# Two fused network blocks in float32 on one core: small tiles moved to pools behind the others

## The chip, the cores and the metric

The kernel runs on one NeuronCore of a Trainium2 chip. The metric is the time of one execution on the device, in microseconds (us); the time of a kernel is the median of several executions. Before the change three executions took 3017.45, 3017.50 and 3017.97 us.

## The reference, cut to what matters

Two blocks follow each other on 512 tokens of 1024 features (and 256 tokens of context in the first). All of it is float32.

```python
# block 1 (one layer): modulation, one wide projection, delta-rule heads and window pooling, output product
proj = (rms_norm(x) * (1 + scale) + shift) @ w_in
o    = delta_rule(q, k, v, g, beta)            # 8 heads, chunks of 128 tokens, forward and backward
y    = concat([o * silu(z_dn), pool(u) * silu(z_pool)])
x    = x + gate * (y @ w_out)
# block 2 (two layers l)
h = h + 0.5 * swiglu(rmsnorm(h), w_ff1_in[l], w_ff1_out[l])
h = h + hybrid_mixer(rmsnorm(h), ...)          # attention and a convolution of 31 taps, gated, then w_out
h = h + 0.5 * swiglu(rmsnorm(h), w_ff2_in[l], w_ff2_out[l])
h = h + sigmoid(rmsnorm(h) @ w_ple_gate[l]) * (p[l] @ w_ple_proj[l])
```

Most of the work is dense products of activations with weights.

## The kernel before

**The dense product.** Activations lie with features on the 128 partitions and 512 tokens along the free axis, so one tile is 512 float32 values, 2048 bytes, in each partition. TensorE multiplies them in the type fp32r. To keep float32's accuracy each factor is split into a high and a low part, and one 128 x 128 block of weights costs three matmuls of 512 columns (`mm3`, L153 to L158):

```python
    nc.tensor.matmul(ps, lhsT=wh, rhs=xh, start=start, stop=False)   # L156
    nc.tensor.matmul(ps, lhsT=wh, rhs=xl, start=False, stop=False)   # L157
    nc.tensor.matmul(ps, lhsT=wl, rhs=xh, start=False, stop=stop)    # L158
```

The weights (`lhsT`) are loaded into the array, one weight load per matmul; the activations (`rhs`, here called the moving operand) stream through it.

**The weights.** The class Stream brings them in the order of their use, 8 blocks (512 KB) to a DMA into a tile `wraw` (three buffers, L98 and L99), and splits 4 blocks at a time: ACT casts the high part `whi` (L108), DVE subtracts for the low part `wlo` (L109), three buffers each. So 12 matmuls of `mm3` go with one cast and one subtraction, and 24 with one DMA.

**The order.** [...] Block 1 projects and runs the heads one after another; the head before is worked on while the next one is projected (the letters of `STEPS`), then comes the pooling half (`TAIL`), then the output product (`wo`, L1501). Block 2 is, for each of two layers: a first feed-forward (products into `pj`, then per half eight products into `fo`, L352), the mixer, a second feed-forward, and the `ple` product with its gates. Short matmuls in plain float32 (128 columns, for the delta rule and the attention) run between the dense ones in block 1's heads and in block 2's attention.

**Moving operands of the dense products, by name.** `xh`, `xl` (pool `xp` of the whole kernel) are what most of block 2's products into `pj` and all projections `px` of block 1 read. `gh`, `gl` (pool `gp` of block 2, L341 and L342) feed `fo`. `nh`, `nl` (pool `mp` of block 2) take the place of `xh`, `xl` in one feed-forward only, the first one of layer 1 (`prep` with `alt=True`, L640): there the same lines of code multiply with operands that lie elsewhere. `mh`, `ml`, `oh`, `ol`, `ph`, `pl` lie in `gp`, `yh`, `yl` in `mp`. In block 1 `os` (L1489, split at L1494), `ysp`, `yl` and `dsp` feed `wo` and `py`; they lie in its pool `b1c`.

**Where tiles lie.** A pool hands out a fixed stretch of each partition's memory; pools follow each other in the order in which they are opened, and each tile's size is rounded up to 32 bytes. The pools of the whole kernel (`cp`, `wp`, `hp`, `xp`, L1516 to L1519) end at byte 97,792 of the partition, which is 191 x 512. There the pools of block 1 begin, and after block 1 has ended those of block 2, over the same bytes. The built program lists these places (start byte, and its remainder by 512):

| tiles | pool | start bytes | remainder by 512 |
|---|---|---|---|
| `wraw`, `whi`, `wlo` | wp | 24,064 to 46,592 | 0 |
| `xh`, `xl` | xp | 65,024 to 95,744 | 0 |
| `nh`, `nl`, `yh`, `yl` (block 2) | mp | 131,488 to 162,208 | 416 |
| `gh`, `gl`, `mh`, `ml`, `oh`, `ol`, `ph`, `pl` | gp | 164,256 to 207,264 | 416 |
| temporaries `fa`, `fb` and others, tag `t` | tp | 213,408 to 223,648 | 416 |
| `R` (block 2) | b2c | 114,880 and 116,928 | 192 |
| `os`, `ysp`, `dsp`, `yl` (tags P, Q, QK) | b1c | 120,672 to 151,392 | 352 |
| `os` (tags E and B, two operands) | b1c | 178,656 to 188,384 | 480 |

The remainders come from small tiles in front. In block 2 the pool `cp` (L182) mixes tiles of 512 bytes and more with tiles of 16 and 32 bytes (`fv`, `fr`, `ts`, `Rt`, `sm`, `lv`, `lr`, 13 buffers of 32 bytes each, together 416), and the pools `mp`, `gp` and `tp` follow it. In block 1 `cp` (L803) mixes likewise (`par1`, `modv`, the gate columns, the padded inputs `u0` to `u3` of 3096 bytes and others), and `tp` (L804) follows it. A weight block inside `whi` or `wlo` starts at a multiple of 512.

Of the kernel before, what the change touches and what calls it, by code (L numbers as in the profile page):

```python
# [7 lines left out]
F32 = mybir.dt.float32  # L8
F32R = mybir.dt.float32r
# [4 lines left out]
P = 128  # L14
S = 512
D = 1024
KD = D // P
# [3 lines left out]
GRP = 8  # L21
UNIT = 4
# [60 lines left out]
class Stream:  # L83
    """Weight tiles in the order of their use: loads of GRP tiles, split in units of UNIT tiles."""
# [40 lines left out]
    def group(self, dst):  # L125
        """the next GRP tiles as they are"""
        assert self.i % GRP == 0
        self.nc.sync.dma_start(dst, self.dram[self.i // GRP])
        self.i += GRP
# [31 lines left out]
def split_scaled(nc, hi, lo, src, scale):  # L161
    """hi + lo == src * scale (scale: a value per partition)."""
    nc.scalar.activation(hi, src, AF.Copy, scale=scale)
    nc.vector.scalar_tensor_tensor(lo, src, scale, hi.bitcast(F32), op0=ALU.mult, op1=ALU.subtract)
# [12 lines left out]
def block2(tc, kk, W, h, xp, x0, sq0, p_t, par, out_t):  # L177
    """h: 8 tiles [128, 512] (features on partitions), short of the factor 1 / rms of the block before.
    x0: the first operand, split. sq0: the sums of squares for that factor and for the first norm."""
    nc = tc.nc  # L180
    with ExitStack() as ctx:
# [3 lines left out]
        tp = ctx.enter_context(tc.tile_pool(name="b2t", bufs=1))  # L185
        acc = ctx.enter_context(tc.tile_pool(name="b2a", bufs=BANKS2[0], space=PSUM))
# [18 lines left out]
        # second operands of the scores, double buffered, for the two heads of a pair:  # L205
        # upper q and ones; lower k and both parts of the decay sums
# [9 lines left out]
        # mt[q, k] = NEG where k > q  # L216
# [60 lines left out]
        def token_sums(sq):  # L277
            """means of squares with a token per partition, [128, chunk]"""
            ps = paux("ts", (P, 8))
            for t in range(4):  # L280
                nc.tensor.matmul(ps[:, 2 * t:2 * t + 2], lhsT=sq[:, t * P:t * P + P], rhs=kk.ones[1024][:, 0:2],
                                 start=True, stop=True)
            return ps[:, ::2]

        def token_rstd(r, v):
            s = cp.tile([P, 4], F32, tag="ts", name="ts", bufs=2)
            nc.scalar.activation(s, v, AF.Sqrt)
            nc.vector.reciprocal(r, s)
            nc.vector.scalar_tensor_tensor(s, r, -0.5, r, op0=ALU.mult, op1=ALU.mult)
            nc.vector.tensor_tensor(s, v, s, op=ALU.mult)  # L290
            nc.vector.scalar_tensor_tensor(r, s, 1.5, r, op0=ALU.add, op1=ALU.mult)

        def spread(r):
            """from a token per partition to tokens along the free axis of every partition"""
# [6 lines left out]
        def first_norm():  # L301
            """1 / rms of the block before times the first norm's factor; and the former for h"""
            v = [cp.tile([P, 4], F32, name=f"fv{i}") for i in range(2)]
            r = [cp.tile([P, 4], F32, name=f"fr{i}") for i in range(2)]
# [55 lines left out]
        def mixer(l, after):  # L360
# [8 lines left out]
            def qk_steps(hp, qk1):  # L369
                """for either head: (upper | lower) q and (upper | upper) k"""  # L370
# [56 lines left out]
            def taps(n):  # L427
                """the next n of the products that are possible by now"""
# [7 lines left out]
            def heads(hp, qk1, filler):  # L436
                """heads 2 hp and 2 hp + 1, each in its half of the partitions"""
# [7 lines left out]
                for qb in range(4):  # L445
# [9 lines left out]
                    for i, ps in enumerate(pss):  # L455
                        o = ps[:, :n]
                        nc.tensor.matmul(ps[:, qs], lhsT=kk.identr, rhs=maskr, start=False, stop=True)
                        sm = cp.tile([P, 4], F32, tag="sm", name="sm", bufs=4)
# [32 lines left out]
            # token sums of squares per partition, for the token-major values  # L491
# [4 lines left out]
            Rt = cp.tile([P, 8], F32, tag="Rt", name="Rt")  # L496
            rstd(Rt, pst)
            # v, token-major
# [12 lines left out]
            # forget gates: rows 0..7 and again 64..71  # L511
# [9 lines left out]
            # -log_sigmoid = ln(1 + exp(-|z|)) - min(z, 0)  # L521
# [35 lines left out]
            # the merge: gates run ahead of the two parts  # L557
# [84 lines left out]
        v = cp.tile([P, 4], F32, name="lv")  # L642
        r = cp.tile([P, 4], F32, name="lr")
# [10 lines left out]
def blocks(v, n):  # L654
    """[..., n * 128] -> [128, ... * n]"""
# [35 lines left out]
NX = 512  # L691
# [7 lines left out]
# (shift, scale) blocks that are computed together  # L699
# [98 lines left out]
def block1(tc, kk, W, h, xp, hp, xt, ctxt, par1, po, rcnt, prep2):  # L798
    """Fills h (8 tiles [128, 512]) with the block's output before its final norm is applied, times the
    final gain; prep2(m) is called for each one. Returns the sums of squares for both norms."""  # L800
    nc = tc.nc
    with ExitStack() as ctx:
        cp = ctx.enter_context(tc.tile_pool(name="b1c", bufs=1))  # L803
        tp = ctx.enter_context(tc.tile_pool(name="b1t", bufs=1))  # L804
        dp = ctx.enter_context(tc.tile_pool(name="b1d", bufs=2, space=bass.MemoryType.DRAM))
# [4 lines left out]
        par = cp.tile([P, par1.shape[1]], F32, name="par1")  # L810
# [28 lines left out]
        # ---- constants  # L839
# [6 lines left out]
        for d in range(2):  # L846
            t = tmp("tri", (P, P))
            # d = 0: 1 where row <= col; d = 1: 1 where row >= col
# [7 lines left out]
        for b in (16, 32, 64):  # L856
            # -1 on the two off-diagonal blocks of every pair of b x b blocks
# [13 lines left out]
        # row selector: column r picks rows r and 64 + r  # L871
        zs = cp.tile([80, 16], F32R, name="zsel")
# [16 lines left out]
        # ---- modulation vectors, [128, block, (x, ctx)]  # L889
        # (x, ctx) of every input tile, the last ones filled up to a column tile  # L890
        cm = cp.tile([P, 2 * KD + 30], F32, name="cm")
# [3 lines left out]
        # sums over the four column tiles, whose first two rows count  # L895
        sum4 = cp.tile([P, 2], F32, name="sum4")
# [4 lines left out]
        modv = cp.tile([P, 24, 2], F32, name="modv")  # L901

        def modulation(bs, tiled, tiles):
            """four blocks; tiled: with the inputs spread over four column tiles"""
# [19 lines left out]
        # ---- load x, ctx; sums of squares; scale by the reciprocal rms  # L924
# [21 lines left out]
        def newton(r, v, s):  # L946
            """r = 1 / sqrt(v) to float32's accuracy from an estimate r; s: scratch"""
# [4 lines left out]
        def squares(i):  # L952
            R, n = raw[i], (NX, NCX)[i]
            sq = cp.tile([P, NT + 6], F32, tag=f"u{n // NX}", name="sq")[:, :n]
# [24 lines left out]
        A = cp.tile([P, KD, 2], F32, name="A")  # L979
# [48 lines left out]
        # ---- gates: per token on partitions, [128, chunk, 2 directions x 8 heads]  # L1028
# [9 lines left out]
        def gcol(name):  # L1038
            return cp.tile([P, 6, 16], F32, name=name)
# [3 lines left out]
        ea = cp.tile([P, 16], F32, name="ea")  # L1043
# [24 lines left out]
        Gr = cp.tile([P, 6, 16], F32R, name="Gr")  # L1068
# [10 lines left out]
        # ---- per head  # L1079
        # tokens with two columns of zeros around each sequence: ctx from 2 on, x from 260 on  # L1080
        us = {}
        for i in range(4):
            u = cp.tile([P, NT + 6], F32, tag=f"u{i}", name=f"u{i}")
# [5 lines left out]
        def conv5(px, pc, blk, dst):  # L1089
            """centred convolution over tokens, then silu; dst: [128, NT + 2] (a gap after ctx) or [128, NX],  # L1090
            None: left in the input's place"""
# [10 lines left out]
            t = tp.tile([P, NT + 2], F32, tag="cv", name="cv", bufs=1)[:, :n]  # L1102
# [14 lines left out]
        def k_in(hd):  # L1117
# [10 lines left out]
            ss = cp.tile([P, 4, 6], F32, tag="ssk", name="ssk", bufs=2)  # L1128
# [14 lines left out]
            # gamma and its product with the decay to the chunk's end, [128, chunk, direction]  # L1143
            st.ga = cp.tile([P, 2, 6, 2], F32, tag="ga", name="ga", bufs=2)
# [18 lines left out]
        def q_in(st):  # L1163
# [9 lines left out]
            st.sq = cp.tile([P, 4], F32, tag="ssq", name="ssq", bufs=2)  # L1173
            # 128 eps (|q|^2 + eps)
            nc.vector.tensor_scalar(st.sq, pq[:, 0:8:2], EPS, P * EPS, op0=ALU.add, op1=ALU.mult)

        def pre(st):
            """The triangular systems' matrices, forward above the diagonal and backward below it, and the
            inverses of their 16 x 16 diagonal blocks."""
# [30 lines left out]
            # one block per partition: forward ones transposed from 0 on, backward ones from 64 on  # L1210
# [9 lines left out]
            # X: the forward inverse's transpose, the backward inverse  # L1220
            XT = tmp("XT")[0:112, :256].rearrange("p (r c) -> p r c", c=16)
            nc.vector.tensor_copy(XT, X.rearrange("p r c -> p c r"))
            # inverses (backward | forward) and their transposes (forward | backward)
# [20 lines left out]
        def merge(st):  # L1244
            """Doubles the inverted blocks three times. With the blocks 1 and 2 of a pair, for B upper triangular
            (forward) and lower triangular (backward) in one matrix:
            P12 = -P11 B12 P22 (forward), P21 = -P22 B21 P11 (backward), Q: the transposes."""
            for b in (16, 32, 64):
                g = 64 // b

                def alt(t, c):
                    """columns of blocks 1 of each pair from the first matrix, of blocks 2 from the second"""
# [78 lines left out]
        def finish(st, z):  # L1331
            f = cp.tile([P, 4, 4], F32, tag="f", name="f", bufs=2)
# [44 lines left out]
        # ---- pooling half  # L1377
# [5 lines left out]
        ups = [cp.tile([P, NT + 6], F32, tag=f"u{2 + e}", name="up")[:, :640].rearrange("p (r c) -> p r c", c=80) for e in range(2)]  # L1383
# [4 lines left out]
        rns = [tp.tile([P, 14, 64], F32, tag="cv", name="rn0", bufs=1),  # L1388
# [12 lines left out]
        def pool_in(g):  # L1401
            """differences to the window means of group g"""
# [3 lines left out]
            for e in range(2):  # L1406
# [3 lines left out]
                # along the columns: into the middle rows  # L1410
# [11 lines left out]
                if w == 16:  # L1422
                    # all eight rows
# [5 lines left out]
                else:  # L1429
                    # row r of the grid: row r + 4 of rows, row r + 3 of the partial sums  # L1430
# [55 lines left out]
        # ---- delta-rule half  # L1486
# [90 lines left out]
```

## Time and profile before

| what | value |
|---|---|
| median of three executions | 3017.5 us |
| lowest and highest | 3017.45 and 3017.97 us |
| span of the profiled execution (first to last instruction) | 3016.3 us |
| PE (matmuls) busy | 2970.0 us, 98% of the span, 13,980 instructions |
| PEld (weight loads) busy | 2395.5 us, 79% |
| DVE busy | 1916.6 us, 64% |
| ACT busy | 1302.3 us, 43% |
| TensorE clock granted, mean over the span | 0.995 of full speed |
| DMA | 268.77 MB, mean 89 GB/s |

The profile is of one execution; what lies between its span and the median is 1.2 us. Matmuls overlap in the profile: each has a duration of some 0.39 us, but in a dense run a new one starts every 0.23 us. What a matmul costs is therefore read from the distance between starts, not from its duration. A plain float32 matmul appears as two instructions (two passes), an fp32r one as one.

### The profile page before, as it was taken

What the parts mean: (1) busy time and instruction counts of PE and PEld (TensorE: products, weight loads), DVE (VectorE), ACT (ScalarE), POOL (GpSimd) and SP (SyncE); (2) the same over time, 40 slices, a digit from 0 to 9 for tenths busy, and PEclk for the clock granted to TensorE, in tenths of its full rate; (3) what the DMA queues carried; (4) which work ended last, traced back from release to release, by engine and by line L of the source; (5) the groups of instructions that cost most, each with busy time, mean ns of one, the idle gap of its engine ahead of it and who ended that gap; (6) DMA issues with size and microseconds to landing.
All of it is one profiled execution on the core that took longest, in us unless ns stands there. A gap on an engine that the chain in (4) does not pass through costs nothing.

```text
span 3016.3 us, 37957 instructions
## 1 busy us (share of the span) xinstructions
PE 2970.0 (98%) x13980; PEld 2395.5 (79%) x13980; DVE 1916.6 (64%) x3778; ACT 1302.3 (43%) x2395; POOL 48.4 (2%) x105
## 2 busy tenths in 40 slices
PE   7999999999999999999999999999999999999998
PEld 4888887777888887688888878888887688888886
DVE  5788888777534469886543447434469886543446
ACT  5667666435323335544332335323335544432333
POOL 1000000000000000000000000000000000000000
PEclk9999999999999999999999999999999999999999
DMA  5211113232232232133333333323222123233322
GB/s 199 66 46 45 52 51 110 91 91 89 93 98 97 92 98 78 50 92 97 94 95 98 98 98 93 96 91 98 91 93 89 50 85 98 93 96 98 98 91 84
DMA packets 112971, 268.77 MB, mean 89 GB/s; under 512 B 43537, under 2 KB 47121, under 8 KB 112785
## 3 DMA queue, kind: packets, MB, share of 16 engines
q1 hardware_dynamic: 111760, 266.28, 28.3%
q8 instruction: 110, 1.80, 0.2%
q14 instruction: 77, 0.62, 0.1%
q0 software_dynamic: 1024, 0.07, 0.0%
HBM read 262.17 MB, written 4.06 MB: 88 GB/s over the span
## 4 chain that ended last, share of the span: by engine, by line
PE 95%; DVE 2%; ACT 2%; issue 1%; DMA 0%; DVEq 0%; SPq 0%; ACTq 0%
PE pj L158 17%; PE pj L157 17%; PE pj L156 17%; PE fo L158 5%; PE fo L157 5%; PE fo L156 5%; PE px L156 3%; PE px L157 3%; PE px L158 3%; PE o L484 1%; PE wo L157 1%; PE wo L158 1%; PE mP L1266 1%; PE mX L1261 1%; PE wo L156 1%; PE chn L1313 1%
## 5 line engine op out<-in xcount | busy, mean ns | idle before, releaser
L108 ACT CAST whi<-wraw 128x512 fp32r<-128x512 f32 x914 | 566.6, 620 | 1191.9 <-PE pj L157 712.2
L109 DVE TENSOR_TENSOR wlo<-wraw,whi 128x512 fp32r<-128x512 f32 x914 | 627.1, 687 | 465.9 <-ACT whi L108 441.8
L157 PE MATMUL pj<-xl,whi 128*128 128x512 f32 x1712 | 673.0, 393 | 0.0
L156 PE MATMUL pj<-xh,whi 128*128 128x512 f32 x1712 | 670.7, 392 | 0.9 <-DVE h L1502 0.9
L158 PE MATMUL pj<-xh,wlo 128*128 128x512 f32 x1712 | 670.0, 391 | 0.0
L158 PEld LDWEIGHTS pj<-xh,wlo 128*128 128x128 f32 x1712 | 322.1, 188 | 68.1 <-issue 2.3
L157 PEld LDWEIGHTS pj<-xl,whi 128*128 128x128 f32 x1712 | 322.2, 188 | 67.9 <-issue 2.7
L156 PEld LDWEIGHTS pj<-xh,whi 128*128 128x128 f32 x1712 | 322.4, 188 | 66.8 <-ACT whi L108 1.3
L158 PE MATMUL fo<-gh,wlo 128*128 128x512 f32 x704 | 279.1, 396 | 0.0
L157 PE MATMUL fo<-gl,whi 128*128 128x512 f32 x704 | 279.1, 396 | 0.0
L156 PE MATMUL fo<-gh,whi 128*128 128x512 f32 x704 | 279.0, 396 | 0.0
L418 DVE SCALAR_TENSOR_TENSOR cy<-ca,par,cy 128x489 f32<-128x489 f32 (+17 forms) x240 | 169.6, 729 | 1.5
L157 PE MATMUL px<-xl,whi 128*128 128x512 f32 x392 | 160.4, 409 | 0.0
L158 PE MATMUL px<-xh,wlo 128*128 128x512 f32 x392 | 160.0, 408 | 0.0
L156 PE MATMUL px<-xh,whi 128*128 128x512 f32 x392 | 159.3, 406 | 0.0
L157 PEld LDWEIGHTS fo<-gl,whi 128*128 128x128 f32 x704 | 132.6, 188 | 32.3
L156 PEld LDWEIGHTS fo<-gh,whi 128*128 128x128 f32 x704 | 132.6, 188 | 32.3
L158 PEld LDWEIGHTS fo<-gh,wlo 128*128 128x128 f32 x704 | 132.6, 188 | 32.3
L339 DVE TENSOR_TENSOR fb<-pj,R 128x512 f32<-128x512 f32 x88 | 60.8, 691 | 131.5 <-PE pj L158 131.5
L336 DVE TENSOR_TENSOR fa<-pj,R 128x512 f32<-128x512 f32 x88 | 60.8, 691 | 127.4 <-PE pj L158 125.5
L156 PE MATMUL pj<-nh,whi 128*128 128x512 f32 x352 | 140.0, 398 | 0.0
L157 PE MATMUL pj<-nl,whi 128*128 128x512 f32 x352 | 139.5, 396 | 0.0
(431 smaller groups left out, 4499.0 us busy)
## 6 DMA issues: line engine op xcount, KB each, us to landing
wraw<-in_w_dram SPq DMA_DIRECT2D x465, 512.0 KB
mw<-in_w_dram SPq DMA_DIRECT2D x16, 512.0 KB
raw<-in_xt_dram SPq DMA_DIRECT2D x8, 256.0 KB
h<-in_xt_dram SPq DMA_DIRECT2D x8, 256.0 KB
out_dram<-fin SPq DMA_DIRECT2D x8, 256.0 KB
rawc<-in_ctxt_dram SPq DMA_DIRECT2D x2, 512.0 KB
db<-B SPq DMA_DIRECT2D x64, 6.0 KB
Pm<-dq SPq DMA_DIRECT2D x64, 12.0 KB
```

The source lines that it names most:

```text
L108: nc.scalar.copy(hi, src)
L109: nc.vector.tensor_tensor(lo, src, hi.bitcast(F32), op=ALU.subtract)
L156: nc.tensor.matmul(ps, lhsT=wh, rhs=xh, start=start, stop=False)
L157: nc.tensor.matmul(ps, lhsT=wh, rhs=xl, start=False, stop=False)
L158: nc.tensor.matmul(ps, lhsT=wl, rhs=xh, start=False, stop=stop)
L336: nc.vector.tensor_tensor(a, pa, R, op=ALU.mult)
L339: nc.vector.tensor_tensor(b, pb, R, op=ALU.mult)
L418: nc.vector.scalar_tensor_tensor(yy[:, s:], ca[cb][:, :S - s], pcol("conv_w", l, cb, j), yy[:, s:], op0=ALU.mult, op1=ALU.add)
L484: nc.tensor.matmul(po_[r, kb * P:], lhsT=vt[kb][:, hp * P + 64 * i:hp * P + 64 * i + 64], rhs=pts[i], start=kb == 0, stop=kb == 3)
L1261: nc.tensor.matmul(pX[:, o], lhsT=st.B[:, m0 + m], rhs=alt(st.Q, m0 + m), start=True, stop=True)
L1266: nc.tensor.matmul(pP[:, o], lhsT=Xt[:, m], rhs=alt(st.P, m0 + m), start=True, stop=True)
L1313: nc.tensor.matmul(pa, lhsT=st.kN[:, c], rhs=y2, start=True, stop=True)
```

## The change

Two new pools `sp` are opened behind the other SBUF pools of block 1 and of block 2, and every tile whose size in a partition is no multiple of 512 bytes takes its memory from there. The instructions, their order and the sizes of all tiles stay as they were. (Comments and docstrings are also dropped from the file; they are left out here.)

```diff
 def block2(tc, kk, W, h, xp, x0, sq0, p_t, par, out_t):
         tp = ctx.enter_context(tc.tile_pool(name="b2t", bufs=1))
+        sp = ctx.enter_context(tc.tile_pool(name="b2s", bufs=1))
...
-            s = cp.tile([P, 4], F32, tag="ts", name="ts", bufs=2)
+            s = sp.tile([P, 4], F32, tag="ts", name="ts", bufs=2)
...
-            v = [cp.tile([P, 4], F32, name=f"fv{i}") for i in range(2)]
-            r = [cp.tile([P, 4], F32, name=f"fr{i}") for i in range(2)]
+            v = [sp.tile([P, 4], F32, name=f"fv{i}") for i in range(2)]
+            r = [sp.tile([P, 4], F32, name=f"fr{i}") for i in range(2)]
...
-                        sm = cp.tile([P, 4], F32, tag="sm", name="sm", bufs=4)
+                        sm = sp.tile([P, 4], F32, tag="sm", name="sm", bufs=4)
...
-            Rt = cp.tile([P, 8], F32, tag="Rt", name="Rt")
+            Rt = sp.tile([P, 8], F32, tag="Rt", name="Rt")
...
-        v = cp.tile([P, 4], F32, name="lv")
-        r = cp.tile([P, 4], F32, name="lr")
+        v = sp.tile([P, 4], F32, name="lv")
+        r = sp.tile([P, 4], F32, name="lr")
...
 def block1(tc, kk, W, h, xp, hp, xt, ctxt, par1, po, rcnt, prep2):
         tp = ctx.enter_context(tc.tile_pool(name="b1t", bufs=1))
+        sp = ctx.enter_context(tc.tile_pool(name="b1o", bufs=1))
...
-        par = cp.tile([P, par1.shape[1]], F32, name="par1")
+        par = sp.tile([P, par1.shape[1]], F32, name="par1")
...
-            u = cp.tile([P, NT + 6], F32, tag=f"u{i}", name=f"u{i}")
+            u = sp.tile([P, NT + 6], F32, tag=f"u{i}", name=f"u{i}")
...
-            t = tp.tile([P, NT + 2], F32, tag="cv", name="cv", bufs=1)[:, :n]
+            t = sp.tile([P, NT + 2], F32, tag="cv", name="cv", bufs=1)[:, :n]
...
```

In block 1 the same is done to `zsel`, `cm`, `sum4`, `modv`, `sq`, `A`, the gate columns, `ea`, `Gr`, `ssk`, `ga`, `ssq`, `f`, `up` and `rn0`. The pools of the whole kernel are not touched.

## Rows read from the trace of the kernel before

**Rows 1.** The page: span, busy time of the engines, chain that ended last by engine.
```profile
span 3016.3 us, 37957 instructions
...
PE 2970.0 (98%) x13980; PEld 2395.5 (79%) x13980; DVE 1916.6 (64%) x3778; ACT 1302.3 (43%) x2395; POOL 48.4 (2%) x105
...
PE 95%; DVE 2%; ACT 2%; issue 1%; DMA 0%; DVEq 0%; SPq 0%; ACTq 0%
```
**Rows 2.** The page's costliest groups: xcount | busy us, mean ns | idle before, releaser.
```profile
L108 ACT CAST whi<-wraw 128x512 fp32r<-128x512 f32 x914 | 566.6, 620 | 1191.9 <-PE pj L157 712.2
L109 DVE TENSOR_TENSOR wlo<-wraw,whi 128x512 fp32r<-128x512 f32 x914 | 627.1, 687 | 465.9 <-ACT whi L108 441.8
L157 PE MATMUL pj<-xl,whi 128*128 128x512 f32 x1712 | 673.0, 393 | 0.0
...
L157 PE MATMUL fo<-gl,whi 128*128 128x512 f32 x704 | 279.1, 396 | 0.0
...
L157 PE MATMUL pj<-nl,whi 128*128 128x512 f32 x352 | 139.5, 396 | 0.0
```
**Rows 3.** Timeline of PE, layer 0's first feed-forward: start us, duration, instruction.
```profile
780.05 0.39 PE L157 MATMUL pj<-xl,whi 128*128 128x512 f32 x1
...
839.89 0.39 PE L157 MATMUL pj<-xl,whi 128*128 128x512 f32 x1
```
**Rows 4.** Timeline of PE, layer 1's first feed-forward.
```profile
1899.72 0.39 PE L157 MATMUL pj<-nl,whi 128*128 128x512 f32 x1
...
1979.85 0.40 PE L157 MATMUL pj<-nl,whi 128*128 128x512 f32 x1
```
**Rows 5.** Windows holding rows 3 and 4: us, busy (xcount) by engine, PEclk, DMA share, GB/s.
```profile
760.00:840.00 80.00, 80.00 (x359) 66.37 (x358) 41.64 (x65) 27.41 (x45) 0.00 (x0) 1.00 0.29 93
...
1880.00:1990.00 110.00, 110.00 (x471) 88.41 (x470) 53.05 (x81) 37.35 (x60) 0.00 (x0) 1.00 0.29 92
```
**Rows 6.** Timeline of PE, the products into fo of layer 0's first feed-forward.
```profile
859.87 0.39 PE L157 MATMUL fo<-gl,whi 128*128 128x512 f32 x1
...
899.93 0.39 PE L157 MATMUL fo<-gl,whi 128*128 128x512 f32 x1
```
**Rows 7.** Timeline of PE, block 1's output product.
```profile
700.05 0.40 PE L158 MATMUL wo<-os,wlo 128*128 128x512 f32 x1
...
723.87 0.39 PE L158 MATMUL wo<-os,wlo 128*128 128x512 f32 x1
```
**Rows 8.** Timeline of PE, the switch from wo to px in block 1's pooling half.
```profile
606.36 0.39 PE L156 MATMUL px<-xh,whi 128*128 128x512 f32 x1
...
608.67 0.39 PE L157 MATMUL px<-xl,whi 128*128 128x512 f32 x1
```
**Rows 9.** Groups of PE by line and form: xcount | busy us, mean ns | idle before.
```profile
L157 PE MATMUL px<-xl,whi 128*128 128x512 f32 x392 | 160.4, 409 | 0.0
...
L157 PE MATMUL pj<-ml,whi 128*128 128x512 f32 x128 | 50.7, 396 | 0.0
...
L156 PE MATMUL wo<-ysp,whi 128*128 128x512 f32 x64 | 25.6, 410 | 1.2 <-ACT ysp L168 1.1
...
L157 PE MATMUL pj<-yl,whi 128*128 128x512 f32 x64 | 25.4, 396 | 0.0
...
L157 PE MATMUL pj<-ol,whi 128*128 128x512 f32 x64 | 25.4, 396 | 0.0
...
L158 PE MATMUL wo<-os,wlo 128*128 128x512 f32 x64 | 25.3, 395 | 0.0
```
**Rows 10.** Timeline of PE: runs of plain float32 passes, weights off and on a multiple of 512.
```profile
301.32 0.83 PE L1266 MATMUL mP<-Pm,Xt 128*128 128x128 f32 x6
...
729.46 0.95 PE L281 MATMUL ts<-ones,sq 128*128 128x2 f32 x8
```
**Rows 11.** Timeline of PE where block 2 begins.
```profile
726.67 0.39 PE L158 MATMUL wo<-os,wlo 128*128 128x512 f32 x1
727.99 0.47 PE L156 MATMUL pj<-xh,whi 128*128 128x512 f32 x1 [0.94 <-DVE h L1502]
```

More of the change, by code (lines that the diff above doesn't have):

```diff
@@ L870, in block1 @@
         nc.vector.memset(onesm, 1.0)
-        zs = cp.tile([80, 16], F32R, name="zsel")
+        zs = sp.tile([80, 16], F32R, name="zsel")
         zt = tmp("zt", (80, 16))
@@ L887, in block1 @@
             DD.append((lt, xx))
-        cm = cp.tile([P, 2 * KD + 30], F32, name="cm")
+        cm = sp.tile([P, 2 * KD + 30], F32, name="cm")
         nc.vector.memset(cm, 0.0)
@@ L894, in block1 @@
             nc.scalar.activation(cm[:, i:2 * KD:2], pcol(nme, 0, 8), AF.Silu)
-        sum4 = cp.tile([P, 2], F32, name="sum4")
+        sum4 = sp.tile([P, 2], F32, name="sum4")
         nc.gpsimd.memset(sum4, 0.0)
@@ L900, in block1 @@
                                     pattern=[[-1, 2]], channel_multiplier=1)
-        modv = cp.tile([P, 24, 2], F32, name="modv")
+        modv = sp.tile([P, 24, 2], F32, name="modv")
         def modulation(bs, tiled, tiles):
@@ L953, in squares @@
             R, n = raw[i], (NX, NCX)[i]
-            sq = cp.tile([P, NT + 6], F32, tag=f"u{n // NX}", name="sq")[:, :n]
+            sq = sp.tile([P, NT + 6], F32, tag=f"u{n // NX}", name="sq")[:, :n]
             nc.scalar.activation(sq, R[0], AF.Square)
@@ L977, in normalize @@
                 nc.vector.tensor_tensor(R[m], R[m], pr, op=ALU.mult)
-        A = cp.tile([P, KD, 2], F32, name="A")
+        A = sp.tile([P, KD, 2], F32, name="A")
         xh, xl, ch_, cl_ = [], [], [], []
@@ L1038, in gcol @@
         def gcol(name):
-            return cp.tile([P, 6, 16], F32, name=name)
+            return sp.tile([P, 6, 16], F32, name=name)
         z, e, g_ = (tmp(n)[:, :96].rearrange("p (c r) -> p c r", r=16) for n in ("gz", "ge", "gg"))
         beta = gcol("beta")
-        ea = cp.tile([P, 16], F32, name="ea")
+        ea = sp.tile([P, 16], F32, name="ea")
         nc.scalar.activation(ea, pcol("a_log", 0, 16), AF.Exp)
@@ L1067, in block1 @@
         nc.vector.memset(G2, 0.0)
-        Gr = cp.tile([P, 6, 16], F32R, name="Gr")
+        Gr = sp.tile([P, 6, 16], F32R, name="Gr")
         nc.vector.tensor_copy(Gr, G)
@@ L1127, in k_in @@
                 scaled("kN", st.kN[:, a:b], pt[:, :(b - a) * P].rearrange("p (c r) -> p c r", r=P))
-            ss = cp.tile([P, 4, 6], F32, tag="ssk", name="ssk", bufs=2)
+            ss = sp.tile([P, 4, 6], F32, tag="ssk", name="ssk", bufs=2)
             junk = tmp("junk")
@@ L1142, in k_in @@
             nc.vector.reciprocal(ss[:, 2], ss[:, 0])
-            st.ga = cp.tile([P, 2, 6, 2], F32, tag="ga", name="ga", bufs=2)
+            st.ga = sp.tile([P, 2, 6, 2], F32, tag="ga", name="ga", bufs=2)
             rec = ss[:, 2].unsqueeze(2).to_broadcast([P, 6, 2])
@@ L1172, in q_in @@
                 nc.tensor.matmul(pq[:, 2 * c:2 * c + 2], lhsT=qs[:, c * P:c * P + P], rhs=onesm[:, 0:2], start=True, stop=True)
-            st.sq = cp.tile([P, 4], F32, tag="ssq", name="ssq", bufs=2)
+            st.sq = sp.tile([P, 4], F32, tag="ssq", name="ssq", bufs=2)
             nc.vector.tensor_scalar(st.sq, pq[:, 0:8:2], EPS, P * EPS, op0=ALU.add, op1=ALU.mult)
@@ L1331, in finish @@
         def finish(st, z):
-            f = cp.tile([P, 4, 4], F32, tag="f", name="f", bufs=2)
+            f = sp.tile([P, 4, 4], F32, tag="f", name="f", bufs=2)
             junk = tmp("junk2")
@@ L1381, in block1 @@
             h.append(t)
-        ups = [cp.tile([P, NT + 6], F32, tag=f"u{2 + e}", name="up")[:, :640].rearrange("p (r c) -> p r c", c=80) for e in range(2)]
+        ups = [sp.tile([P, NT + 6], F32, tag=f"u{2 + e}", name="up")[:, :640].rearrange("p (r c) -> p r c", c=80) for e in range(2)]
         cns = [cp.tile([P, 6, P], F32, tag="E", name="cn", bufs=2).rearrange("p c r -> p (c r)")[:, :640].rearrange("p (r c) -> p r c", c=80)
@@ L1387, in block1 @@
         rows = qt[:, :1024].rearrange("p (r c) -> p r c", c=64)
-        rns = [tp.tile([P, 14, 64], F32, tag="cv", name="rn0", bufs=1),
+        rns = [sp.tile([P, 14, 64], F32, tag="cv", name="rn0", bufs=1),
                cp.tile([P, 14, 64], F32, tag="B", name="rn1", bufs=2)]
```

## The prediction

> **What bounds the kernel now.** I read the page first. PE is busy for 98% of the span and 95% of the chain that ended last is PE [rows 1], so the time is the number of matmuls times the distance between their starts. Most of them are the three-part dense products of 512 columns [rows 2]; ACT's casts and DVE's subtractions idle before them, waiting for PE to give buffers back [rows 2]. A change that alters no instruction can act here only through the pace of PE, so next I read the timeline for that pace, taking distances between starts and counting the matmuls between two rows.
>
> In the first feed-forward of layer 0 (moving operand `xh`, `xl`, remainder 0) 264 matmuls start between the two rows: 59.84 us / 264 = 226.7 ns [rows 3]. In the first feed-forward of layer 1 the same lines, with weights from the same buffers, take their moving operand from `nh`, `nl` (remainder 416): 80.13 us / 342 = 234.3 ns [rows 4]. [...] `fo` reads `gh`, `gl` (416 too) and has the same pace: 40.06 us / 171 = 234.3 ns [rows 6]. Block 1's output product reads `os` (mostly 352) and has another: 23.82 us / 102 = 233.5 ns [rows 7]. Two remainders, two paces, and 0 is fastest. I call 226.7 ns the locked pace, since a run does not begin with it: after the switch from `wo` to `px` (remainder 0) the first ten steps take 2.31 us instead of 2.27 [rows 8], 0.04 us lost.
>
> **The change part by part.** Where tiles go: the pools of both blocks begin at 97,792 = 191 x 512. With the small tiles moved behind, every tile in front of them is a multiple of 512 bytes long, so all tiles of `b2c`, `mp`, `gp`, `tp` and of block 1's first two pools get remainder 0. In block 2 the moved tiles are 13 x 32 = 416 bytes, just the remainder that is there now.
>
> Gain, block 2, at 234.3 - 226.7 = 7.6 ns for each matmul off the grid:
> - `fo`: 3 x 704 = 2112 [rows 2] x 7.6 ns = 16.1 us.
> - `nh`, `nl`: 3 x 352 = 1056 [rows 2] x 7.6 ns = 8.0 us.
> - `mh`, `ml`: 3 x 128 = 384 [rows 9] x 7.6 ns = 2.9 us.
> - `oh`, `yh`: 3 x 64 each [rows 9]; `ph`: by the code 2 layers x 8 columns x 2 blocks x 3 = 96; together 480 x 7.6 ns = 3.6 us. These come in runs of 12 or 6 between runs of 24 on `xh`; I give them the price of their remainder.
>
> Gain, block 1: `wo` 192 from `os` and 192 from the pooling half [rows 9], `py` 48 by the code; 432 x (233.5 - 226.7) = 2.9 us. Some follow waits for `ysp` [rows 9], so I take off 0.7 us.
>
> Switches: the 30 or so places of block 2 where a full run on `xh` follows a run off the grid lose up to 0.04 us each [rows 8], 1.2 us; I take 1.0.
>
> Sum: 16.1 + 8.0 + 2.9 + 3.6 + 2.2 + 1.0 = 33.8 us, all on PE and so on the path.
>
> Costed at nothing, with the cover:
> - Weights arriving faster than now: at the locked pace 12 matmuls take 2.72 us, and the cast and the subtraction they need 0.62 + 0.69 us [rows 2]. The runs on `xh` already hold this pace, at 93 GB/s [rows 5], so the supply is there; without it PE would wait at each unit.
> - `px` in block 1 (3 x 392 [rows 9]) and the 256-column products: operands lie on the grid before and after. They stand in short runs between plain float32 passes, so they are rarely locked. Bounds: if the neighbours' new places let all of them lock, at most 1176 x 7.6 ns = 8.9 us gained; if these disturb the longer runs, some 3 us lost. I take 0, since operands and order stay.
> - Plain float32 passes of 128 columns: six with weights off the grid (`Xt`) span 0.83 us, eight with weights on it (`sq`) and only 2 columns 0.95 us [rows 10]; without the last one's tail of some 0.28 us and 0.16 us that is 0.11 us per pass in both. No gain, no loss; bound 1 ns either way.
> - ACT and DVE: the subtraction, all on the grid, takes 687 ns [rows 2]; both engines have slack [rows 1].
> - New neighbours in memory: a tile of block 2 waits for the tile of block 1 that held its bytes. By the sizes, block 2's moved tiles (bytes 225,280 on) land on block 1's `cv` and its neighbours, last used in the pooling half, far before block 2 begins; `par1` and `modv`, used to block 1's end, fall under `gl10`, written some 100 us into block 2. So nothing new is late at the boundary, where PE idles 0.94 us now [rows 11]; without that cover it would be a few us, once.
>
> The profiled execution (span 3016.3) stands 1.2 us below the median. 3016.3 - 33.8 = 2982.5 us of span, 2983.7 us as a median. What is late next: PE still, at its locked pace.
>
> [...]
>
> **The rivals.**
>
> *The remainder is not the cause (no change).* All slow operands also lie above byte 120,000 and all fast ones below 98,000, and `xh` shares its remainder by 2048 (1536) with the weight buffers, which no moved tile will. If the region decides, or the place by 2048, the products keep their pace: 3017.5 us. For it: before, the two properties are never apart. Against it: `os` and `nh` lie over the same bytes around 145,000, yet run at 233.5 and 234.3 ns [rows 4, 7], as their remainders differ; and four weight blocks in turn start at all four multiples of 512 within 2048, while the run on `xh` stays at 226.7 ns [rows 3]. [...]
>
> *Only the long runs lock (part of it).* `fo`, `nh` and `mh` give 27.0 us, the interleaved ones and block 1 nothing: 2990.5 us. For it: a run needs some ten steps [rows 8]. Against: the neighbours of the interleaved ones would be on the grid too, so the lock need not break. This lies within my range.
>
> *All on one grid, and the lock breaks (slower).* Now DVE and ACT read and write `fa`, `fb` and `R` at 416 and 192 while `xh` streams at 0; afterwards they touch the same remainders as PE. If that shifts PE's reads, the 5136 matmuls on `xh`, `xl` [rows 2] fall to 234.3 ns, 39 us lost, and the others gain nothing: 3056 us. It decides from the point where more than 45% of the roughly 9600 dense matmuls run unlocked (33 us to win against 39 + 33). Against it: `wraw`, `whi` and `wlo` are on the grid already, and their casts and subtractions, 22 of each within the 264 matmuls of rows 3, leave the pace alone.
>
> **How the numbers follow.** Forecast with its partial form: 0.88. No change: 0.09. Slower: 0.03. Predicted 2983.7 us. Range: down to 2974 us if `px` locks too (33.8 + 8.9 = 42.7 us); up to 2993 us if only the long runs gain, less 2.5 us for `px`. It leaves out the two other rivals and little of the forecast. A measurement of this kernel can tell about 0.2% (6 us) from no change: faster by more 0.88, within 0.09, slower 0.03.
>
> **What would show it.** The starts of `fo` and of `nh`, `nl` should be 226.7 ns apart, those of `wo` too, and `xh` unchanged; PE's busy time should fall by about 34 us with the same counts; DVE's and ACT's busy times and the mean of a plain float32 pass should stay. The prediction is wrong if `fo` or `nh` keeps 234 ns, if `xh` leaves 226.7 ns, or if a new wait stands where block 2 begins.

## The result, and the profile after

| | before | after |
|---|---|---|
| median of four runs each, us | 3017.47 | 2982.72 |
| lowest and highest, us | 3017.39 and 3017.97 | 2981.87 and 2983.71 |
| span of the profiled execution, us | 3016.3 | 2980.9 |
| PE busy, us | 2970.0 | 2935.6 |

The ratio is 0.9886, with a 95% interval of 0.9873 to 0.9899. The kernel became 34.8 us faster; 33.8 us had been forecast, a median of 2983.7 us with a range of 2974 to 2993.

The page of the kernel after: its span, the busy time of each engine, and the chain that ended last.

```profile
span 2980.9 us, 37957 instructions
PE 2935.6 (98%) x13980; PEld 2393.3 (80%) x13980; DVE 1914.2 (64%) x3778; ACT 1302.4 (44%) x2395; POOL 48.1 (2%) x105
PE 95%; DVE 2%; ACT 2%; issue 1%; DMA 0%; DVEq 0%; SPq 0%; ACTq 0%
L108 ACT CAST whi<-wraw 128x512 fp32r<-128x512 f32 x914 | 567.0, 621 | 1158.5 <-PE pj L157 700.3
L109 DVE TENSOR_TENSOR wlo<-wraw,whi 128x512 fp32r<-128x512 f32 x914 | 627.4, 687 | 449.4 <-ACT whi L108 427.0
```

The counts of PE, DVE and ACT are those of [rows 1]. PE's busy time fell by 34.4 us, nearly the whole gain, and PE still makes up 95% of the chain. DVE and ACT moved by 2.4 and 0.1 us, and their two largest groups have the same means as in [rows 2]. So PE does the same work in less time.

Where it does so is read from the timeline of PE, kernel after (start, duration, engine, line, operation), at the places of [rows 3, 4, 6, 7, 8, 11]. Two lines make a stretch.

```profile
604.56 0.39 PE L156 MATMUL px<-xh,whi 128*128 128x512 f32 x1
...
606.83 0.39 PE L157 MATMUL px<-xl,whi 128*128 128x512 f32 x1
...
690.39 0.39 PE L158 MATMUL wo<-os,wlo 128*128 128x512 f32 x1
...
713.51 0.39 PE L158 MATMUL wo<-os,wlo 128*128 128x512 f32 x1
...
723.03 0.39 PE L158 MATMUL wo<-os,wlo 128*128 128x512 f32 x1
724.35 0.47 PE L156 MATMUL pj<-xh,whi 128*128 128x512 f32 x1 [0.94 <-DVE h L1504]
...
779.85 0.39 PE L157 MATMUL pj<-xl,whi 128*128 128x512 f32 x1
...
839.69 0.39 PE L157 MATMUL pj<-xl,whi 128*128 128x512 f32 x1
...
860.09 0.39 PE L157 MATMUL fo<-gl,whi 128*128 128x512 f32 x1
...
899.53 0.39 PE L157 MATMUL fo<-gl,whi 128*128 128x512 f32 x1
...
1869.62 0.39 PE L157 MATMUL pj<-nl,whi 128*128 128x512 f32 x1
...
1949.87 0.39 PE L157 MATMUL pj<-nl,whi 128*128 128x512 f32 x1
```

| stretch | working | pace after, ns | pace before, ns |
|---|---|---|---|
| `wo` from `os` | 23.12 us / 102 | 226.7 | 233.5 [rows 7] |
| `xh`, `xl`, layer 0 | 59.84 us / 264 | 226.7 | 226.7 [rows 3] |
| `fo` from `gh`, `gl` | 39.44 us / 174 | 226.7 | 234.3 [rows 6] |
| `nh`, `nl`, layer 1 | 80.25 us / 354 | 226.7 | 234.3 [rows 4] |

Each of these dense stretches now has the pace that only `xh` had before. The ten steps after the switch from `wo` to `px` take 2.27 us where they took 2.31 [rows 8]. The idle time ahead of block 2 is 0.94 us, unchanged [rows 11]. The groups of PE's matmuls, shapes kept apart (count | busy us, mean ns of one | idle us), answer to [rows 9]:

```profile
L157 PE MATMUL px<-xl,whi 128*128 128x512 f32 x392 | 160.3, 409 | 0.0
L157 PE MATMUL pj<-ml,whi 128*128 128x512 f32 x128 | 49.8, 389 | 0.0
L157 PE MATMUL pj<-ol,whi 128*128 128x512 f32 x64 | 24.9, 389 | 0.0
L157 PE MATMUL pj<-yl,whi 128*128 128x512 f32 x64 | 24.9, 389 | 0.0
```

In these two kernels a locked matmul shows a duration of 389 ns and one off the lock some 394 to 398 (before, `fo` and `ml` 396 [rows 2, 9]). So `ml`, `ol` and `yl` are locked, though the last two come in short runs between runs on `xh`. The mean of `px` stays at 409, but it mixes two kinds: 320 of its 1176 matmuls are the first of a run, with 450 ns each, while in both kernels those from the eleventh of a run on have 389 or 390.

Summed over all matmuls, from the distance of each one's end to the end before it, the gain divides like this:

| term | forecast, us | measured, us |
|---|---|---|
| `fo` | 16.1 | 16.05 |
| all projections of block 2, with the switches | 8.0 + 2.9 + 3.6 + 1.0 = 15.5 | 15.22 |
| `wo` and `py` | 2.2 | 2.22 + 0.15 |
| `px` | 0 | 0.57 |
| ahead of block 1's first projection (47.40 to 46.62 us) | 0 | 0.8 |
| the last eight passes of `ts`, at the end of the kernel | 0 | 0.74 |

The remaining groups moved by at most 0.3 us each, in both directions. The products alone thus gave 34.2 us. The last two rows cannot be credited to the change. In the kernels of the experiments below the first `px` starts anywhere from 46.75 to 48.21 us (47.86 before, 47.08 after), so the start varies by more than 0.8 us. The last passes of `ts` follow a wait of PE for DVE, 3.6 us before and 3.7 us after; before, they ran at a granted clock of 0.50 and took 1.84 us, after, at a mean of 0.90, 1.06 us; in sweep_a, which has the small tiles moved too, they took 1.84 us again.

### The profile page after: what moved, and what is told of

It is laid out like the page before. It is cut to its first block, busy times and chain, and to the rows that moved or that the text cites. A ratio compares the mean times of both kernels' runs of the same rounds, so it can differ in the third digit from the quotient of the medians.

```text
span 2980.9 us, 37957 instructions
## 1 busy us (share of the span) xinstructions
PE 2935.6 (98%) x13980; PEld 2393.3 (80%) x13980; DVE 1914.2 (64%) x3778; ACT 1302.4 (44%) x2395; POOL 48.1 (2%) x105
## 4 chain that ended last, share of the span: by engine, by line
PE 95%; DVE 2%; ACT 2%; issue 1%; DMA 0%; DVEq 0%; SPq 0%; ACTq 0%
PE pj L158 17%; PE pj L156 17%; PE pj L157 17%; PE fo L156 5%; PE fo L158 5%; PE fo L157 5%; PE px L156 3%; PE px L157 3%; PE px L158 3%; PE o L485 1%; PE wo L157 1%; PE mP L1268 1%; PE mX L1263 1%; PE wo L158 1%; PE wo L156 1%; PE chn L1315 1%
## 5 line engine op out<-in xcount | busy, mean ns | idle before, releaser
L157 PE MATMUL pj<-xl,whi 128*128 128x512 f32 x1712 | 673.3, 393 | 0.0
L156 PE MATMUL pj<-xh,whi 128*128 128x512 f32 x1712 | 671.1, 392 | 0.9 <-DVE h L1504 0.9
L158 PE MATMUL pj<-xh,wlo 128*128 128x512 f32 x1712 | 670.2, 391 | 0.0
L158 PEld LDWEIGHTS pj<-xh,wlo 128*128 128x128 f32 x1712 | 322.2, 188 | 67.8 <-issue 2.3
L157 PEld LDWEIGHTS pj<-xl,whi 128*128 128x128 f32 x1712 | 322.3, 188 | 66.8 <-issue 2.7
L156 PEld LDWEIGHTS pj<-xh,whi 128*128 128x128 f32 x1712 | 322.4, 188 | 65.9 <-ACT whi L108 1.3
L157 PE MATMUL fo<-gl,whi 128*128 128x512 f32 x704 | 274.1, 389 | 0.0
L158 PE MATMUL fo<-gh,wlo 128*128 128x512 f32 x704 | 274.1, 389 | 0.0
L156 PE MATMUL fo<-gh,whi 128*128 128x512 f32 x704 | 274.1, 389 | 0.0
L157 PE MATMUL px<-xl,whi 128*128 128x512 f32 x392 | 160.3, 409 | 0.0
L158 PE MATMUL px<-xh,wlo 128*128 128x512 f32 x392 | 160.0, 408 | 0.0
L156 PE MATMUL px<-xh,whi 128*128 128x512 f32 x392 | 159.2, 406 | 0.0
L158 PEld LDWEIGHTS fo<-gh,wlo 128*128 128x128 f32 x704 | 132.2, 188 | 27.4
L157 PEld LDWEIGHTS fo<-gl,whi 128*128 128x128 f32 x704 | 132.2, 188 | 27.4
L156 PEld LDWEIGHTS fo<-gh,whi 128*128 128x128 f32 x704 | 132.2, 188 | 27.3
L156 PE MATMUL pj<-nh,whi 128*128 128x512 f32 x352 | 137.5, 391 | 0.0
L157 PE MATMUL pj<-nl,whi 128*128 128x512 f32 x352 | 137.2, 390 | 0.0
```

## Experiments

The gain is where it was forecast. The reason is less sure: the forecast read it from two remainders, 0 and 416 (352 in block 1), and the change alters many things together: where the operands lie, where the temporaries of DVE and ACT lie, which pool holds the small tiles, and which region each tile is in. My theory was that the remainder of the moving operand sets the pace. The rivals: that DVE's and ACT's places matter; that the region does; that what counts is not the moving operand's own place but its distance from the weights. All edits are to the kernel after, but for the last but one, which is to the kernel before. A *pad* is a tile that only takes up bytes, as `padw` in the first diff of that kind below; GpSimd sets each to zero once, which the diffs leave out.

### Each block's half alone

One kernel has the change in block 2 alone, the other in block 1 alone:

```diff
 # block2_only: block 1 as before
-            u = sp.tile([P, NT + 6], F32, tag=f"u{i}", name=f"u{i}")
+            u = cp.tile([P, NT + 6], F32, tag=f"u{i}", name=f"u{i}")
...
 # block1_only: block 2 as before
-            Rt = sp.tile([P, 8], F32, tag="Rt", name="Rt")
+            Rt = cp.tile([P, 8], F32, tag="Rt", name="Rt")
...
```

> Small tiles moved behind in block 2 alone; block 1 laid out as before. Grid theory (the place of the moving operand by 512 sets the pace of each dense product by itself): fo, nh, mh, oh, yh and ph start 226.7 ns apart, wo keeps 233.5 ns, block 2's gain of 31 to 33 us stays and block 1's 2.5 us are missing, so some 2985 us. Neighbour theory (the gain hangs on the whole memory layout, both blocks together): clearly less than 30 us gained, above 2990 us.

> Small tiles moved behind in block 1 alone; block 2 as before. Grid theory: only wo and py gain, 2 to 3 us, some 3015 us, with wo at 226.7 ns and fo at 234.3 ns. Neighbour theory: a time more than 5 us away from that.

Block 2 alone: 2985.69 us, ratio 0.9896 (0.9881 to 0.991). Block 1 alone: 3014.45 us, ratio 0.999 (0.9981 to 1.0). The kernel before had 3016.92 us on that chip, so the halves are 31.2 and 2.5 us (the second at the edge of what its interval can tell from nothing), and together 33.7. Groups of PE, first with block 2 alone, then with block 1 alone:

```profile
L157 PE MATMUL fo<-gl,whi 128*128 128x512 f32 x704 | 273.9, 389 | 0.0
...
L158 PE MATMUL wo<-os,wlo 128*128 128x512 f32 x64 | 25.3, 395 | 0.0
```

```profile
L157 PE MATMUL fo<-gl,whi 128*128 128x512 f32 x704 | 279.1, 396 | 0.0
...
L158 PE MATMUL wo<-os,wlo 128*128 128x512 f32 x64 | 24.9, 389 | 0.0
```

In each kernel only the products of the block whose tiles moved are at 389 ns. The halves add up, to within 1.1 us of the 34.8 us of the whole change.

### The weights moved, and then everything moved

In the first kernel the operands stay at remainder 0 and only the split weights, `whi` and `wlo`, go to 416. A pad of 416 bytes lies ahead of their pool and one of 96 behind it, which puts all that follows back to 0. The second kernel leaves the 96 bytes out, so that weights, operands and temporaries all lie at 416.

```diff
-        hi = self.pool.tile([P, UNIT * P], F32R, tag="whi", name="whi", bufs=3)
-        lo = self.pool.tile([P, UNIT * P], F32R, tag="wlo", name="wlo", bufs=3)
+        hi = self.split_pool.tile([P, UNIT * P], F32R, tag="whi", name="whi", bufs=3)
+        lo = self.split_pool.tile([P, UNIT * P], F32R, tag="wlo", name="wlo", bufs=3)
...
+        padw = ctx.enter_context(tc.tile_pool(name="padw", bufs=1)).tile([P, 104], F32, name="padw")
+        vp = ctx.enter_context(tc.tile_pool(name="vp", bufs=1))
+        # the next line in weights_416 alone
+        padh = ctx.enter_context(tc.tile_pool(name="padh", bufs=1)).tile([P, 24], F32, name="padh")
...
```

> The kernel after, with whi and wlo alone shifted to remainder 416, every moving operand still at 0. Theory of the operand's own place (the moving operand has to start on a multiple of 512): nothing changes, 226.7 ns, 2983 us. Theory of the difference (what counts is how the moving operand's start stands to the weights' start): every fp32r product falls to a pace above 226.7 ns, 231 to 235 ns, that is 4 to 8 ns on some 9600 products, 40 to 77 us more, 3022 to 3060 us.

> The kernel after, with weights, xh, nh, gh, the context operand and both blocks' pools all shifted together to remainder 416. Theory of the difference: the pace stays 226.7 ns and the time 2983 us. Theory of the operand's own place: every product takes 234.3 ns, some 73 us more, 3056 us.

With the weights alone at 416: 3044.46 us, ratio 1.009 (1.007 to 1.0111), slower than before the change. With everything at 416: 2983.08 us, ratio 0.9887 (0.9867 to 0.9907), as fast as the change. The page's busy times, a window with the columns of [rows 5], and PE's timeline in `fo` and in a run on `xh`, weights alone moved:

```profile
PE 2998.4 (99%) x13980; PEld 2391.2 (79%) x13980; DVE 1923.8 (63%) x3778; ACT 1302.2 (43%) x2395; POOL 48.2 (2%) x107
...
860.00:910.00 50.00, 50.00 (x216) 40.23 (x215) 16.62 (x25) 10.80 (x19) 0.00 (x0) 1.00 0.28 95
```

```profile
870.25 0.39 PE L157 MATMUL fo<-gl,whi 128*128 128x512 f32 x1
...
905.25 0.39 PE L157 MATMUL fo<-gl,whi 128*128 128x512 f32 x1
...
929.75 0.39 PE L157 MATMUL pj<-xl,whi 128*128 128x512 f32 x1
...
1009.55 0.39 PE L157 MATMUL pj<-xl,whi 128*128 128x512 f32 x1
```

The same window, and `fo`, with everything moved:

```profile
860.00:910.00 50.00, 50.00 (x223) 41.39 (x222) 16.88 (x25) 11.82 (x19) 0.00 (x0) 1.00 0.31 99
...
870.06 0.39 PE L157 MATMUL fo<-gl,whi 128*128 128x512 f32 x1
...
905.42 0.39 PE L157 MATMUL fo<-gl,whi 128*128 128x512 f32 x1
```

With the weights alone moved, `fo` takes 35.00 us / 150 = 233.3 ns and the run on `xh` 79.80 us / 342 = 233.3 ns; PE's busy time is 62.8 us above that of the kernel after. With everything moved, `fo` takes 35.36 us / 156 = 226.7 ns. The granted clock is 1.00 in both. An operand at 416 is thus neither slow nor fast by itself. It is slow against weights at 0, as before the change, and fast against weights at 416; an operand at 0 is slow against weights at 416. What sets the pace is the difference between the two starts. My theory, which put it down to the operand alone, fell here.

### The temporaries of DVE and ACT

The operands stay at 0 and pads move only the temporaries: block 2's `tp` goes back to 416 and `R` to 192.

```diff
+        pad2 = ctx.enter_context(tc.tile_pool(name="pad2", bufs=1)).tile([P, 48], F32, name="pad2")
         # then b2c; the same with 80 columns ahead of mp and 104 ahead of tp
```

> The kernel after, with block 2's temporaries (fa, fb and the others, remainder 416) and R (192) put back to their old remainders while weights and moving operands stay at 0. If only PE's two operands matter: 226.7 ns everywhere, 2983 us, DVE's mean for fa and fb 691 ns as before. If the places of what ACT and DVE touch had a part in the gain: fo and nh slower than 226.7 ns, and some us more.

2983.43 us, ratio 0.989 (0.9861 to 0.9919). Groups of this kernel:

```profile
L157 PE MATMUL fo<-gl,whi 128*128 128x512 f32 x704 | 273.9, 389 | 0.0
...
L346 DVE TENSOR_TENSOR fb<-pj,R 128x512 f32<-128x512 f32 x88 | 60.8, 691 | 129.3 <-PE pj L158 129.3
```

PE keeps its pace, and the DVE group has the same 691 ns as in the kernel after, where `R` and `fb` lie at 0:

```profile
L340 DVE TENSOR_TENSOR fb<-pj,R 128x512 f32<-128x512 f32 x88 | 60.8, 691 | 129.3 <-PE pj L158 129.3
```

At these places, 416 and 192, block 2's temporaries have no part in the gain.

### Which differences lock

Three kernels put pads between the pools of the kernel after, so that up to three differences are seen in each. `xh` is in a pool of its own, `nh` and `yh` in `mp`, `gh` and `mh` in `gp`.

```diff
 # sweep_a: xh at 256, nh and yh at 128, gh at 64
+        padx = ctx.enter_context(tc.tile_pool(name="padx", bufs=1)).tile([P, 64], F32, name="padx")
+        pad2m = ctx.enter_context(tc.tile_pool(name="pad2m", bufs=1)).tile([P, 32], F32, name="pad2m")
+        pad2g = ctx.enter_context(tc.tile_pool(name="pad2g", bufs=1)).tile([P, 112], F32, name="pad2g")
...
 # sweep_b: xh at 32, nh and yh at 192, gh at 384
 # sweep_c: xh at 0, nh and yh at 224, gh at 320
```

> Three differences between the moving operand's and the weights' start in one kernel: xh, xl 256, nh and yh 128, gh (fo, mh, oh, ph) 64. If the period is 512, all three run slower than 226.7 ns (231 to 235), some 3040 to 3055 us. If it is 256, xh alone keeps 226.7 ns and nh and fo are slow: about 2983 + 9 (nh, yh) + 21 (fo, mh, oh, ph) = 3013 us. If it is 128, nh keeps 226.7 ns too and the time is some 3004 us. If it is 64, all stay at 226.7 ns, 2983 us. A pace under 226.7 ns at one of the three would show a better place than the change's own.

> Three more differences: xh, xl 32, nh and yh 192, gh 384. With a period of 512 or 256 all are slow (231 to 235 ns), 3040 to 3060 us; gh at 384 shares its rest by 256 with nh of the run before (128), so the two should have the same pace. With a period of 128, gh alone runs at 226.7 ns. If a coarser step of 64 were all that counts, nh and gh run at 226.7 ns and xh alone is slow, some 3020 us.

> xh at 0, nh and yh at a difference of 224, gh at 320, which is 64 by 256. With a period of 256, fo has the pace and the pattern that it had at 64 (some 229 ns, and some of its matmuls at 226) and not the 232 to 234 ns of the others. nh at 224: slow, 229 to 235 ns. Time 2983 + 3 x 704 x 2.4 ns (5) + some 2 for mh, oh, ph + 1248 x 3 to 8 ns (4 to 10), 2994 to 3000 us. If the period were 512, fo could have any pace between 226.7 and 235 ns.

One run each: 2997.14, 3042.68 and 3001.2 us. PE's timeline of sweep_a, in `fo`, a run on `xh`, and the run on `nh`:

```profile
870.13 0.39 PE L157 MATMUL fo<-gl,whi 128*128 128x512 f32 x1
...
905.15 0.39 PE L157 MATMUL fo<-gl,whi 128*128 128x512 f32 x1
...
929.71 0.39 PE L157 MATMUL pj<-xl,whi 128*128 128x512 f32 x1
...
1009.95 0.39 PE L157 MATMUL pj<-xl,whi 128*128 128x512 f32 x1
...
1899.79 0.40 PE L157 MATMUL pj<-nl,whi 128*128 128x512 f32 x1
...
1959.75 0.40 PE L157 MATMUL pj<-nl,whi 128*128 128x512 f32 x1
```

At 64: 35.02 us / 153 = 228.9 ns. At 256: 80.24 us / 354 = 226.7 ns, the locked pace, so a multiple of 512 is not needed. At 128: 59.96 us / 258 = 232.4 ns. The run was shorter than the expected 3013 us because 64 bytes cost less than thought. In sweep_c, `fo` at 320, which is 64 more than 256:

```profile
870.24 0.39 PE L157 MATMUL fo<-gl,whi 128*128 128x512 f32 x1
...
905.26 0.39 PE L157 MATMUL fo<-gl,whi 128*128 128x512 f32 x1
```

Again 35.02 us / 153 = 228.9 ns, as at 64, which is a second sign of a period of 256; this run came 1 us above its expected 2994 to 3000. In sweep_b none of block 2's long runs locks, and the kernel is slower than before the change. Its runs on `xh` and `nh`:

```profile
929.42 0.39 PE L157 MATMUL pj<-xl,whi 128*128 128x512 f32 x1
...
1009.92 0.40 PE L157 MATMUL pj<-xl,whi 128*128 128x512 f32 x1
...
1899.64 0.40 PE L157 MATMUL pj<-nl,whi 128*128 128x512 f32 x1
...
1959.14 0.39 PE L157 MATMUL pj<-nl,whi 128*128 128x512 f32 x1
```

At 32: 80.50 us / 345 = 233.3 ns. At 192: 59.50 us / 255 = 233.3 ns. Of the eight runs of `fo`, at 384, four have 232.4 ns and four 233.3. The run on `nh` in sweep_c, at 224:

```profile
1899.89 0.40 PE L157 MATMUL pj<-nl,whi 128*128 128x512 f32 x1
...
1959.39 0.40 PE L157 MATMUL pj<-nl,whi 128*128 128x512 f32 x1
```

That is 59.50 us / 255 = 233.3 ns.

Taken together, by the difference of the starts (operand less weights, remainder by 256):

| difference | pace, ns | seen in |
|---|---|---|
| 0 | 226.7 | after; all_416; `xh` at 256 in sweep_a |
| 32 | 233.3 | `xh` in sweep_b |
| 64 | 228.9 | `gh` in sweep_a and, at 320, in sweep_c |
| 96 | 233.3 to 233.5 | weights_416; `os` at 352 before |
| 128 | 232.4, and 233.3 in half the runs of `gh` | `nh` in sweep_a, `gh` at 384 in sweep_b |
| 160 | 234.3 | `nh` and `gh` at 416 before |
| 192 | 233.3 | `nh` in sweep_b |
| 224 | 233.3 | `nh` in sweep_c |

None of these eight is faster than 0. At 128 the same difference gave two paces in different runs, so the difference does not settle everything; what else plays a part was not resolved.

### Two pads, and no tile moved

If the difference is all, the kernel before needs no new pool: 160 bytes ahead of block 1's pools and 96 bytes ahead of `mp` bring most of its operands to the weights' remainder. This is the kernel before with these two pads alone.

```diff
+        pad2 = ctx.enter_context(tc.tile_pool(name="pad2", bufs=1)).tile([P, 24], F32, name="pad2")
         # ahead of mp in block 2
...
+        pad1 = ctx.enter_context(tc.tile_pool(name="pad1", bufs=1)).tile([P, 40], F32, name="pad1")
         # ahead of the pools of block 1
```

> The kernel before, with no tile moved: a pad of 160 bytes in front of block 1's pools and one of 96 bytes between block 2's small tiles and its operands, so that nh, gh and most of block 1's operands stand at 0 like the weights; R stays at 192, two of 16 os operands at 128, the small tiles stay mixed in. Theory of the difference: fo, nh, mh at 226.7 ns, wo close to it, 2983 to 2985 us, as good as the change. If moving the small tiles out of the way were itself worth something, this kernel misses that part of the 35 us.

2982.44 us (2981.94 to 2983.29), ratio 0.9886 (0.9869 to 0.9902), against 2982.72 us for the change. Groups of PE:

```profile
L157 PE MATMUL fo<-gl,whi 128*128 128x512 f32 x704 | 273.9, 389 | 0.0
...
L158 PE MATMUL wo<-os,wlo 128*128 128x512 f32 x64 | 25.0, 390 | 0.0
```

Block 2's products are locked. `wo` takes 228.4 ns on average over its 192 matmuls from `os`, two of whose operands still lie at 128. Collecting the small tiles in a pool of their own is thus worth nothing by itself; it was one way of making the starts agree.

### Only the low half of the weights moved

In the three-part product the lines are `hi` x `whi` (L156), `lo` x `whi` (L157) and `hi` x `wlo` (L158). Here only `wlo` lies at 128, all else at 0. If a matmul is slowed by its own weights, only L158 should be drawn out; if by the weights that load beside it for the next one, only L157, beside which `wlo` loads (in the kernel after, one load of `wlo` takes 0.19 us from 870.30 us on, beside the L157 matmul that starts at 870.29).

```diff
-        lo = self.pool.tile([P, UNIT * P], F32R, tag="wlo", name="wlo", bufs=3)
+        lo = self.lo_pool.tile([P, UNIT * P], F32R, tag="wlo", name="wlo", bufs=3)
...
+        padl = ctx.enter_context(tc.tile_pool(name="padl", bufs=1)).tile([P, 32], F32, name="padl")
+        lp = ctx.enter_context(tc.tile_pool(name="lp", bufs=1))
+        padh = ctx.enter_context(tc.tile_pool(name="padh", bufs=1)).tile([P, 96], F32, name="padh")
...
```

> All moving operands and whi at 0, wlo alone at 128. Whose weights count? If a matmul's pace hangs on the load that runs beside it (the next matmul's weights), the one of L157 is drawn out, beside which wlo is loaded; if on its own weights, that of L158; either way one in three is slow, 3200 x 5.7 ns, some 3000 us. If one such matmul throws the whole run out of step, all three are slow, 230 to 233 ns, some 3015 to 3045 us.

One run: 3024.27 us. Groups of PE by line:

```profile
L158 PE MATMUL fo<-gh,wlo 128*128 128x512 f32 x704 | 279.5, 397 | 0.0
L157 PE MATMUL fo<-gl,whi 128*128 128x512 f32 x704 | 278.8, 396 | 0.0
L156 PE MATMUL fo<-gh,whi 128*128 128x512 f32 x704 | 273.9, 389 | 0.0
```

From the end before to their own end the lines of `fo` take 226.2 (L156), 233.7 (L157) and 233.5 ns (L158). Neither version came out: the matmul beside which the misplaced weights load is drawn out, and so is the one that uses them. The third, which meets neither, keeps its pace. So the cost belongs to the matmuls around a misplaced load and does not spread over the run; which step inside makes it is open. In weights_416 ACT and DVE also wrote the splits at the new place, but with one cast and one subtraction for twelve matmuls they write beside all three lines: by the starts and durations in the trace of the kernel after, the subtractions lie over 25 to 26% of the steps of each line of `fo`, the casts over 21 to 25%. So their writing is not likely to be what draws out two lines and spares the third.

## Why the prediction was right, and where its reason was too narrow

- **PE's pace as the only lever**: right. PE's busy time fell by 34.4 us at the same counts, where "about 34 us" stood (some 0.7 of it in the last passes of `ts`, at a clock of 0.50 before and 0.90 after); the largest change on another engine was DVE's 2.4 us. Clock and DMA share had been the same at 226.7 and at 234.3 ns, 1.00 and 0.29 [rows 5], so the place of the operand was what differed.
- **7.6 ns for each matmul off the grid**: right in size, though "off the grid" was the wrong name for what costs it (below). `fo` gave 16.05 us for 16.1, the projections with their switches 15.22 for 15.5.
- **The interleaved runs at the price of their remainder**: right. `ol` and `yl` are at 389 ns, so the rival "only the long runs lock", at 2990.5 us, fell.
- **Block 1's 2.2 us**: right, 2.37 with `py`, and 2.5 in the run of that half alone.
- **Switches, 1.0 us**: right in size. Block 2's products on `xh` took 0.94 us less in all; it is contained in the 15.22.
- **`px` at nothing, bounds -8.9 and +3**: 0.57 us gained, so taking nothing was sound. Most of its runs, 266 of 320, are one to three matmuls long in both kernels.
- **Plain float32, ACT, DVE, the start of block 2 at nothing**: right; temps_off shows it for the temporaries by themselves, and 0.94 us still stand at the boundary.
- **Not forecast**: 0.8 us ahead of block 1's first projection and 0.74 us in the last passes of `ts`. Both vary from kernel to kernel; the sum of the forecast, 33.8 us, is better set against the 34.2 us of the products.
- **"The remainder is not the cause"**: fell with the result. In the built program of the kernel after, `gh` lies from byte 163,840 on, at remainder 0 by 2048, and most of `os` at remainder 512, while the weights have 1536, and both run at 226.7 ns. (One tile of `os`, at 161,280, did get 1536, against "which no moved tile will".)
- **"All on one grid, and the lock breaks"**: fell. `xh` kept 226.7 ns; all_416, where all share another grid, has it too.

One reading failed although the number held: that a matmul pays 7.6 ns for its operand's own place, "off the grid" of 512 bytes. The rows of before had the weights at one remainder only, so the operand's place and its distance from the weights could not be told apart there. weights_416 and all_416 part them: the distance decides. And sweep_a shows that the grid is 256, not 512. That the number came out all the same is luck in one respect: the change left the weights at remainder 0 and put the operands there, so the narrow reason and the wider one forecast the same time. For weights_416 the narrow one said 2983 us, and 3044.46 were measured.

## What to carry to other kernels

Where a dense product of this kind runs at the limit of PE, compare the distance between starts, on the same lines, for operands from different pools; here 2.2 to 7.6 ns more at the same clock were the sign of misplaced buffers. Bring each moving operand's start and its weights' start to the same remainder by 256: here two pads of 160 and 96 bytes were worth 1.1%, as much as the change. Before a reason is read off a contrast in the trace, ask what was the same in all its rows; here it was the place of the weights.

## What the runs showed of the hardware

- With fp32r operands of 512 columns and a weight load for each matmul, at granted clock 1.00, the pace went from 226.7 ns (difference 0, after) to 234.3 ns (160, before) with the difference of the starts of the moving operand and the weights. It was the same at 0 and 256 (226.7 ns, after and sweep_a) and at 64 and 320 (228.9 ns, sweep_a and sweep_c). Other types and other numbers of columns were not tried.
- The cost did not grow with the misplacement: a difference of 64 bytes cost 2.2 ns a matmul (sweep_a, sweep_c), one of 32 bytes 6.6 ns (sweep_b).
- Within a run the cost stayed local: with only `wlo` misplaced (wlo_128), two of three lines were drawn out by some 7 ns (233.7 and 233.5) and the third kept 226.2 ns.
